# Up projection in Strassen's seven products of half matrices over both token groups, output projection with 512 columns into six open accumulators

## The chip, the cores and the metric

The kernel runs on one core of a Trainium2 chip. The metric is the device time of one execution in microseconds (us); lower is better. The engines are TensorE (PE, with its weight loads as PEld), VectorE (DVE), ScalarE (ACT), GpSimd (POOL) and SyncE (SP); SP's queue issues all the DMAs of this kernel.

## What is computed

One layer of an encoder on two sequences, 512 and 1024 tokens of width 1024, in float32. The kernel puts them together as 1536 tokens. Cut to what matters here:

```python
def trunk(x, ...):
    h = x
    h = h + hybrid_mixer(rmsnorm(h, norm_mix_g), ...)      # attention and gated linear attention
    h = h + sq_relu_mlp(rmsnorm(h, norm_mlp_g), w_up, w_down)
    return rmsnorm(h, norm_final_g)

def hybrid_mixer(u, ...):
    ...
    merged = sigmoid(gate_na) * (na_o @ w_br_na) + sigmoid(gate_gla) * (gla_o @ w_br_gla)
    return merged @ w_out                                  # 1024 x 1024

def sq_relu_mlp(u, w_up, w_down):                          # 1024 x 4096, 4096 x 1024
    return square(relu(u @ w_up)) @ w_down
```

Every matrix product is taken as three: each operand is split into a high part (rounded to float32r) and a low part (what is left), and high x high, high x low and low x high are added up in PSUM.

## The kernel before

The first 900 us (input projections, gated linear attention, neighbourhood attention) are not touched. What follows works on two groups of 768 tokens (`GT`), `for g in range(2)`, and within a group in four stages:

- **Branches** (lines 1311 to 1339): for each of 8 blocks of 128 output columns, four PSUM units of 12 matmuls with 384 columns (two branches, two halves of the tokens, tags d, a, c, b in turn). DVE multiplies each by its gate, adds the two, ACT makes the high part `mh`, DVE the low part `ml`.
- **Output projection** (`wout_mm`, lines 1349 to 1369): for each of six blocks of 128 tokens and four blocks of 256 columns, one PSUM unit of 24 matmuls with 256 columns; DVE adds the result to the row `h`. The last of the four column blocks is taken from a second ring (`dn`) so that a row can be finished, normed (`norm_a`, `norm_b`) and transposed (`x2`, calling `transp_tile`, lines 189 to 198) while the next is computed. `transp_tile` transposes on PE, and ACT and DVE split the result from PSUM into `x2h`, `x2l`.
- **Up projection** (`up`, lines 1394 to 1408): for each of 32 blocks of 128 hidden columns and each half of the tokens, one unit of 24 matmuls with 384 columns in a bank of tag d; ACT takes the Relu out of PSUM, DVE squares it. After every second block `left_factors` forms four sums and differences on DVE and stores seven factors.
- Beside it run the loading of the next group's branch operand (`prep_side`), the sums of down weights (`t_load`, `t_sums`) and, at the end of the second group, the first operands of the down projection (`d_start`).

The **down projection** (`d_all`) already works by Strassen's seven products, reading the factors stored before: 14 steps of 6 units of 24 matmuls with 512 columns, two units ahead prepared by `a_prep` and `b_prep`.

The order of work is written out by hand: the schedule is manual, so each engine runs its instructions in the order in which the program emits them, and the tile framework adds the waits that the data need. Weights come through a ring (`Ring`): SP loads 128x1024 blocks, two of them raw; ACT copies the high part (line 51) and DVE subtracts for the low part (line 52), three of them split. The same split for other tiles is `split_act` (lines 156 and 157). A PSUM tag has a number of banks which its tiles take in turn: two each for tags a, b, c and d here.

Of the kernel before, what the change touches and what calls it, by code (L numbers as in the profile page):

```python
# [79 lines left out]
def tile_trunk(ctx: ExitStack, tc: tile.TileContext, d: dict, y: bass.AP):  # L80
# [64 lines left out]
    for g in range(2):  # L145
        for i in range(8):
            add(f"br{g}.{i}", d["wbr"][i])
        for i in range(3):
            add(f"out{g}.{i}", d["wout"][2 * i], d["wout"][2 * i + 1])
        for i in range(32):  # L150
            add(f"up{g}.{i}", d["wup"][i])
# [880 lines left out]
    axe, ax = right("ax")  # L1032
    x_, h_ = {}, {}

    def big(pool, tag, nm):
        return [pool.tile([128, 8, GT], F32R, tag=tag, bufs=2, name=f"{nm}{c}") for c in "hl"]

    def prep_side(g, pool, tag, xrp, xtag, nb, ahead):

        base = g * GT  # L1040
        x_[g] = big(pool, tag, f"x{g}")
# [4 lines left out]
        def load(e):  # L1046
# [3 lines left out]
            t = xrp.tile([128, 512 if g == 0 else 1024], F32, tag=xtag, bufs=nb, name=f"xr{g}{e}")[:, :512]  # L1050
# [6 lines left out]
        for e in range(ahead):  # L1057
            load(e)
        yield 1
        for e, (kind, i) in enumerate(todo):  # L1060
            t = ld.pop(e)
            if kind == "n":
                sl = slice(i % 2 * 384, i % 2 * 384 + 384)
                split_act(xh[:, i // 2, sl], xl[:, i // 2, sl], t[:, :384])
            else:
# [4 lines left out]
                split_act(xh[:, 4:8, sl], xl[:, 4:8, sl], p.rearrange("p (k t) -> p k t", k=4))  # L1070
            load(e + ahead)
            yield 1

    xre, xr = right("xr")
    pr = prep_side(0, ax, "actA", xr, "xr", 6, 6)
# [10 lines left out]

    p2e = ExitStack()
    p2 = p2e.enter_context(tc.tile_pool(name="p2", bufs=1))
    wde, wd = right("wd")
    dn = Ring(nc, wd, "draw", 1, wd, "dn", 2, [a for _ in range(2) for a in [d["wout"][6], d["wout"][7]]])  # L1090
    dn.load()

    def load_h(g):
        h_[g] = []
        for t in range(6):
            x = p2.tile([128, 1024], F32, tag=f"h{t}", name=f"h{g}{t}")
            SP.dma_start(x, d["x"][g * GT + t * 128:g * GT + (t + 1) * 128])
            h_[g].append(x)

    def load_g(pool, nm, g):  # L1100
        t = pool.tile([128, 1024], F32, tag="gn", name=f"{nm}{g}")
        SP.dma_start(t, d[nm])
        return t
# [13 lines left out]


# [3 lines left out]
    Ad = {(i, kh, g): dr.tile([3, 128, 8, 128], F32, name=f"ad{i}{kh}{g}") for i in LEFT for kh in range(2) for g in range(2)}  # L1122

# [12 lines left out]


# [5 lines left out]
    D1, D2 = [None], [None]  # L1143
    Araw, Ahl, Bhl = {}, {}, {}

    def a_load(u):
        if u < len(units):
            s, t = units[u]
            (i, _, _), kh = steps[s]
            x = D1[0].tile([128, 8, 128], F32R, tag="al", bufs=4, name=f"al{u}")  # L1150
            SP.dma_start(x.bitcast(F32), Ad[i, kh, t // 3][t % 3])
            Araw[u] = x

    def a_prep(u):
        if u < len(units):
            lo = Araw.pop(u)
            hi = D1[0].tile([128, 8, 128], F32R, tag="ah", bufs=4, name=f"ah{u}")
            A.activation(hi, lo.bitcast(F32), AF.Copy)  # L1158
            V.tensor_tensor(lo, lo.bitcast(F32), hi.bitcast(F32), op=ALU.subtract)  # L1159
            Ahl[u] = hi, lo  # L1160

    Braw = {}

    def b_load(s, jj):
# [8 lines left out]
        pool = D1[0] if s == 0 else D2[0]  # L1173
        x = pool.tile([128, 512], F32, tag="bq", bufs=2 if s == 0 else 12, name=f"bq{s}{jj}")
# [3 lines left out]
    def b_prep(s, jj):  # L1178
        if s >= 14:
            return  # L1180
        pool = (D1, D2)[s % 2][0]
        hi = pool.tile([128, 512], F32R, tag="bh", bufs=8, name=f"bh{s}{jj}")
        lo = pool.tile([128, 512], F32R, tag="bl", bufs=8, name=f"bl{s}{jj}")
        split_act(hi, lo, Braw.pop((s, jj)))
        Bhl[s, jj] = hi, lo

    def t_load(j, pool, tags):

        x = [pool.tile([128, 1024], F32, tag=tags[e], bufs=2 if tags[0] == "dnh" else 4, name=f"tq{j}{e}") for e in range(2)]
        for e in range(2):  # L1190
            SP.dma_start(x[e], d["wdn"][2 * j + e])
        return x

    def t_sums(j, x):

        b11, b12, b21, b22 = x[0][:, :512], x[0][:, 512:], x[1][:, :512], x[1][:, 512:]
        V.tensor_tensor(b11, b12, b11, op=ALU.subtract)
        V.tensor_tensor(b12, b22, b12, op=ALU.subtract)
        V.tensor_tensor(b22, b22, b11, op=ALU.subtract)
        V.tensor_tensor(b21, b21, b22, op=ALU.subtract)  # L1200
        for e in range(2):
            SP.dma_start(t_d[2 * j + e], x[e])

    def d_start(part):
        if part == 0:
            for u in range(4):
                a_load(u)
        if part < 4:
            b_load(0, 2 * part)
            b_load(0, 2 * part + 1)  # L1210
        if part > 0:
            b_prep(0, 2 * part - 2)
            b_prep(0, 2 * part - 1)
        if part in (2, 3):
            a_prep(part - 2)

    def d_all():
        hb, acc, ssa = ([], []), {}, {}
        gf = []

        def fin(t, rh, last=False):
# [3 lines left out]
            x = D2[0].tile([128, 1024], F32, tag="x", bufs=3, name=f"xf{t}{rh}")  # L1225
            if rh:
                ss = D2[0].tile([128, 1], F32, tag="ss", bufs=4, name=f"sf{t}")
# [329 lines left out]
```

## Time and profile before

| what | value |
|---|---|
| median of three runs | 2212.14 us (2211.51 to 2214.27) |
| the profiled execution | 2209.44 us |
| its span | 2207.4 us |
| PE busy | 2186.7 us, 99% |
| DVE, ACT busy | 1174.2 us (53%), 782.8 us (35%) |
| branches, per group | 67 us |
| output projection, per group | 73 us |
| up projection, first and second group | 272 and 270 us |
| down projection to the end | 464 us |

Busy time of PE counts the time in which any of its matmuls is in flight. Matmuls are pipelined, so the duration that a matmul's row shows is longer than its distance to the next; what a matmul costs is that distance. Idle time is put down to the instruction that ended it. The stages in the table are stretches of the span, read from the first and last matmuls of their lines.

### The profile page before, as it was taken

How to read it: one execution, taken by the hardware profiler on the slowest of the kernel's cores; microseconds unless marked ns; L12 is line 12 of the kernel's file. 1: busy time of each engine (PE TensorE's matmuls, PEld its weight loads, DVE VectorE, ACT ScalarE, POOL GpSimd, SP SyncE). 2: the span in 40 equal slices, each digit the busy share in tenths (PEclk: the TensorE clock that was granted, in tenths of full speed). 3: DMA queues.
4: the chain of work that ended last, by engine and by line, in shares of the span. 5: the costliest groups of instructions: out<-in, count | busy, mean ns of one | idle time of the engine just before them, and what ended most of it. 6: DMA issues, size and time to landing. Idle time of an engine off the chain costs nothing.

```text
span 2207.4 us, 33043 instructions
## 1 busy us (share of the span) xinstructions
PE 2186.7 (99%) x12864; PEld 2001.6 (91%) x12864; DVE 1174.2 (53%) x2171; ACT 782.8 (35%) x1464; POOL 64.9 (3%) x92
## 2 busy tenths in 40 slices
PE   8999999999999999999999999999999999999998
PEld 8899998888888888899999999999999988888887
DVE  7463876567356666363455454544554544433643
ACT  6622232423355555442322223332222333333542
POOL 1020200000100000000000000000000000000000
PEclk9999999999999999999999999999999999999999
DMA  5342335453377675552477667326777765454653
GB/s 203 124 141 70 102 115 157 100 149 90 118 221 235 203 219 164 198 186 68 164 250 248 215 205 245 105 90 205 227 227 242 248 214 185 166 177 157 210 172 115
DMA packets 256572, 382.45 MB, mean 173 GB/s; under 512 B 35872, under 2 KB 163872, under 8 KB 256416
## 3 DMA queue, kind: packets, MB, share of 16 engines
q1 hardware_dynamic: 256416, 380.35, 53.9%
q8 instruction: 101, 1.65, 0.3%
q14 instruction: 55, 0.45, 0.1%
HBM read 256.54 MB, written 123.73 MB: 172 GB/s over the span
## 4 chain that ended last, share of the span: by engine, by line
PE 90%; issue 7%; DVE 1%; ACT 1%; DMA 1%; POOL 0%; SPq 0%; DVEq 0%; POOLq 0%; ACTq 0%
PE psd L1404 8%; PE psd L1405 8%; PE psd L1403 8%; PE psd L226 7%; PE psd L228 7%; PE psd L227 7%; PE psa L617 3%; PE psd L251 3%; PE psd L252 2%; PE psd L253 2%; PE psd L1364 2%; PE psd L1366 2%; PE psd L1365 2%; PE psc L964 2%; PE psa L1269 2%
## 5 line engine op out<-in xcount | busy, mean ns | idle before, releaser
L52 DVE TENSOR_TENSOR wl<-wr,wh 128x1024 fp32r<-128x1024 f32 x130 | 159.0, 1225 | 149.1 <-ACT wh L51 147.8
L1407 ACT ACTIVATE r<-psd 128x384 f32<-128x384 f32 x128 | 62.9, 492 | 389.8 <-PE psd L1405 389.8
L1408 DVE TENSOR_TENSOR r<-r 128x384 f32<-128x384 f32 x128 | 71.2, 557 | 234.4 <-ACT r L1407 234.4
L51 ACT ACTIVATE wh<-wr 128x1024 fp32r<-128x1024 f32 x130 | 136.7, 1054 | 131.5 <-PE psd L1366 54.0
L226 PE MATMUL psd<-uhiS,wh 128*128 128x512 f32 x448 | 180.6, 403 | 0.8 <-ACT st L288 0.8
L1159 DVE TENSOR_TENSOR al<-al,ah 128x1024 fp32r<-128x1024 f32 x84 | 102.6, 1223 | 148.0 <-ACT ah L1158 148.0
L228 PE MATMUL psd<-uhiS,wl 128*128 128x512 f32 x448 | 175.5, 392 | 0.0
L227 PE MATMUL psd<-uloS,wh 128*128 128x512 f32 x448 | 174.7, 390 | 0.0
L1403 PE MATMUL psd<-n0h,wh 128*128 128x384 f32 x512 | 171.7, 335 | 0.2 <-ACT n0h L197 0.2
L1403 PE MATMUL psd<-n1h,wh 128*128 128x384 f32 x512 | 171.3, 335 | 0.5 <-ACT r L1407 0.3
L1404 PE MATMUL psd<-n0l,wh 128*128 128x384 f32 x512 | 171.1, 334 | 0.3 <-DVE n0l L198 0.3
L1404 PE MATMUL psd<-n1l,wh 128*128 128x384 f32 x512 | 171.1, 334 | 0.3 <-DVE n1l L198 0.3
L1405 PE MATMUL psd<-n0h,wl 128*128 128x384 f32 x512 | 171.1, 334 | 0.0
L1405 PE MATMUL psd<-n1h,wl 128*128 128x384 f32 x512 | 171.0, 334 | 0.0
L1158 ACT ACTIVATE ah<-al 128x1024 fp32r<-128x1024 f32 x84 | 88.6, 1057 | 219.4 <-DMA al<-ads 133.6
L226 PEld LDWEIGHTS psd<-uhiS,wh 128*128 128x128 f32 x448 | 84.2, 188 | 19.0 <-ACT st L288 1.2
L228 PEld LDWEIGHTS psd<-uhiS,wl 128*128 128x128 f32 x448 | 84.0, 188 | 18.5
L227 PEld LDWEIGHTS psd<-uloS,wh 128*128 128x128 f32 x448 | 84.3, 188 | 16.0
L1403 PEld LDWEIGHTS psd<-n1h,wh 128*128 128x128 f32 x512 | 96.1, 188 | 1.1 <-ACT r L1407 0.6
L1404 PEld LDWEIGHTS psd<-n0l,wh 128*128 128x128 f32 x512 | 96.1, 188 | 0.5 <-DVE n0l L198 0.5
L1404 PEld LDWEIGHTS psd<-n1l,wh 128*128 128x128 f32 x512 | 96.1, 188 | 0.5 <-DVE n1l L198 0.5
L1403 PEld LDWEIGHTS psd<-n0h,wh 128*128 128x128 f32 x512 | 96.1, 188 | 0.5 <-ACT n0h L197 0.5
(452 smaller groups left out, 5671.4 us busy)
## 6 DMA issues: line engine op xcount, KB each, us to landing
wr<-in_wup_dram SPq DMA_DIRECT2D x64, 512.0 KB
ads<-s SPq DMA_DIRECT2D x128, 192.0 KB
al<-ads SPq DMA_DIRECT2D x48, 512.0 KB
ad<-r SPq DMA_DIRECT2D x96, 192.0 KB
al<-ad SPq DMA_DIRECT2D x36, 512.0 KB
tq<-in_wdn_dram SPq DMA_DIRECT2D x32, 512.0 KB
t_d<-tq SPq DMA_DIRECT2D x32, 512.0 KB
bq<-t_d SPq DMA_DIRECT2D x64, 256.0 KB
```

The costliest lines, as they stand in the source:

```text
L51: self.nc.scalar.activation(hi, t, AF.Copy)
L52: self.nc.vector.tensor_tensor(lo, t, hi.bitcast(F32), op=ALU.subtract)
L226: T.matmul(p, wh, xh[:, k, sl], start=(k == 0), stop=False)
L227: T.matmul(p, wh, xl[:, k, sl], start=False, stop=False)
L228: T.matmul(p, wl, xh[:, k, sl], start=False, stop=(k == 7))
L251: T.matmul(p[:, :256], xh, wh, start=(k == 0), stop=False)
L1158: A.activation(hi, lo.bitcast(F32), AF.Copy)
L1159: V.tensor_tensor(lo, lo.bitcast(F32), hi.bitcast(F32), op=ALU.subtract)
L1403: T.matmul(p[:, :384], wh[:, es], x2h[:, k, sl], start=(k == 0), stop=False)
L1404: T.matmul(p[:, :384], wh[:, es], x2l[:, k, sl], start=False, stop=False)
L1405: T.matmul(p[:, :384], wl[:, es], x2h[:, k, sl], start=False, stop=(k == 7))
L1408: V.tensor_tensor(r, r, r, op=ALU.mult)
```

## The change

The loop over the two groups is taken apart into branches 0, output 0, branches 1, output 1, and then the up projection of both groups in a row (`up_all`); every group's norm and transposes move into the stage after it, and other work is placed by hooks between blocks (`hook_b0`, `hook_w0`, `hook_b1`, `hook_w1`) and by a table of functions to be called after a given product (`side`).

The output projection (`wout`) holds six PSUM banks open, one for each block of 128 tokens, and passes over the eight rows of weights with 512 columns each; the eight weights are now cut as 256 rows x 512 columns.

The up projection takes a pair of hidden blocks (256 columns) at a time in seven products of half matrices: half of the 1024 rows, one block of 128 columns, half of the tokens. Each is 12 matmuls of 384 columns. The seven left factors of the activations (`factors`, `part`) are made once for each group; the seven right factors of the weights are made in `u_prep`, four products ahead. The sums between products are left to PSUM: product 2 is added onto product 0 in its bank, and so on, and ACT copies the intermediate values out between.

```diff
@@ output projection @@
+    def wout(g, hook):
+        mh, ml = m_[g]
+        for n in range(2):
+            for kq in range(4):
+                wi = where[f"out{g}"] + n * 4 + kq
+                ring.fill(wi)
+                if kq == 0:
+                    acc = [ps("aabbcc"[t]) for t in range(6)]
+                wh, wl = ring.get(wi)
+                for t in range(6):
+                    sl = slice(t * 128, t * 128 + 128)
+                    for kk in range(2):
+                        k = kq * 2 + kk
+                        es = slice(kk * 512, kk * 512 + 512)
+                        a, b = mh[k // 4][:, k % 4, sl], ml[k // 4][:, k % 4, sl]
+                        T.matmul(acc[t], a, wh[:, es], start=(k == 0), stop=False, skip_group_check=True)
+                        T.matmul(acc[t], a, wl[:, es], start=False, stop=False, skip_group_check=True)
+                        T.matmul(acc[t], b, wh[:, es], start=False, stop=(k == 7), skip_group_check=True)
+                    if kq == 3:
+                        hs = h_[g][:, t, n * 512:n * 512 + 512]
+                        V.tensor_tensor(hs, acc[t], hs, op=ALU.add)
+                hook(n * 4 + kq)
@@ norm and transposes, each called from a hook or from side @@
+    def square(g, t, half):
+        s = p2.tile([128, 1], F32, name=f"ss{g}{t}{half}")
+        A.activation(ps("d"), h_[g][:, t, half * 512:half * 512 + 512], AF.Square, accum_out=s)
...
+    def trans_h(g, t):
+        for half in range(2):
+            pt = ps("d")
+            for k in range(4):
+                T.transpose(pt[:, k * 128:(k + 1) * 128], h_[g][:, t, (half * 4 + k) * 128:(half * 4 + k + 1) * 128], ident)
+            A.activation(st_[g][:, t // 3 * 2 + half, :, t % 3 * 128:t % 3 * 128 + 128], pt.rearrange("p (k t) -> p k t", k=4), AF.Copy)
+    def hook_b1(i):
...
+        if i < 6:
+            square(0, i, 1)
+        if 0 < i < 7:
+            norm_h(0, i - 1)
+        if i > 1:
+            trans_h(0, i - 2)
...
@@ factors @@
+    BANK = (0, 1, 0, 2, 0, 1, 0)
+    def part(g, i, src, e):
+        if e == 0:
+            c_[g, i] = q12([2, 4, 384], f"c{g}{i}")
+        c, ks = c_[g, i], slice(2 * e, 2 * e + 2)
+        A.activation(c[:, 0, ks], src, AF.Copy)
+        V.tensor_tensor(c[:, 1, ks], src, c[:, 0, ks].bitcast(F32), op=ALU.subtract)
...
+    def u_prep(n):
+        if n >= 224:
+            return
+        p, i = divmod(n, 7)
+        x = uraw[p]
+        b11, b21, b12, b22 = x[0][:, :512], x[0][:, 512:], x[1][:, :512], x[1][:, 512:]
+        src = (b11, b11, b11, b21, b12, b22, b21)[i]
+        op = {1: (b11, b12, b11), 2: (b11, b22, b11), 4: (b12, b22, b12), 6: (b21, b21, b11)}.get(i)
+        if op:
+            V.tensor_tensor(*op, op=ALU.subtract)
+        if n % 2 == 0:
+            utile[0] = [rngp.tile([128, 1024], F32R, tag=f"w{c}", bufs=3, name=f"uw{c}{n}") for c in "hl"]
...
+        split_act(hi, lo, src)
+        uhl[n] = hi, lo
+        if i == 6:
+            uraw.pop(p)
+            u_load(p + 2)
@@ up projection @@
+    def up_all(side):
+        tail = [None]
+        for n in range(224):
+            p, i = divmod(n, 7)
...
+            b = BANK[i]
+            new = b not in bank
+            if new:
+                bank[b] = ps("abc"[b])[:, :384]
+            wh, wl = uhl.pop(n)
+            c = c_[g, i]
+            for k in range(4):
+                es = slice(k * 128, k * 128 + 128)
+                T.matmul(bank[b], wh[:, es], c[:, 0, k], start=(new and k == 0), stop=False, skip_group_check=True)
+                T.matmul(bank[b], wh[:, es], c[:, 1, k], start=False, stop=False, skip_group_check=True)
+                T.matmul(bank[b], wl[:, es], c[:, 0, k], start=False, stop=(k == 3), skip_group_check=True)
+            if i == 0 and tail[0]:
+                tail[0]()
+            elif i == 1:
+                A.activation(sc[:, :384], bank[0], AF.Copy)
+            elif i == 2:
+                A.activation(sc[:, 384:], bank[1], AF.Copy)
+            elif i == 3:
+                A.activation(sd[:, :384], bank[0], AF.Copy)
+            elif i == 4:
...
+                V.tensor_tensor(re[:, :384], bank[2], sc[:, :384], op=ALU.add)
+                A.activation(re[:, :384], re[:, :384], AF.Relu)
+                A.activation(re[:, :384], re[:, :384], AF.Square)
+            elif i == 5:
+                V.tensor_tensor(ro[:, 384:], bank[0], sc[:, 384:], op=ALU.add)
+            elif i == 6:
+                V.tensor_tensor(ro[:, :384], bank[1], sd[:, :384], op=ALU.add)
+                A.activation(ro, ro, AF.Relu)
+                A.activation(ro, ro, AF.Square)
+                def end(g=g, j=j, re=re, ro=ro, x=bank[0]):
+                    A.activation(re[:, 384:], x, AF.Relu)
+                    A.activation(re[:, 384:], re[:, 384:], AF.Square)
+                    left_factors(g, j, re, ro)
+                tail[0] = end
+            u_prep(n + 4)
+            for f in side.get(n, ()):
+                f()
+        tail[0]()
```

The functions in `side` are: for the first group's last three factors, pair 0; stores, squares, norms and transposes of the second group's rows, pairs 0 to 8; the second group's factors, pairs 9 to 13 (sums and differences of 768 elements) and 15 (twelve calls of `part`); seven rounds of `t_load` and `t_sums`, pairs 10 to 26; the down projection's first operands, pairs 20 to 31. Of the down projection only units 0 and 1 have their left operands before it starts; units 2 and 3 are loaded at its start. The first group's branch operand is loaded four tiles ahead instead of six.

## Rows read from the trace of the kernel before

**Rows 1.** The page: busy time and its share by engine; TensorE's granted clock.

```profile
PE 2186.7 (99%) x12864; PEld 2001.6 (91%) x12864; DVE 1174.2 (53%) x2171; ACT 782.8 (35%) x1464; POOL 64.9 (3%) x92
PEclk9999999999999999999999999999999999999999
```

**Rows 2.** Stretches: length; busy and (instructions) of PE, PEld, DVE, ACT, POOL; clock.

```profile
989.20:1062.20 73.00, 73.00 (x610) 72.74 (x610) 30.23 (x46) 19.17 (x31) 2.77 (x5) 1.00 0.15 51
1062.20:1333.80 271.60, 271.07 (x1578) 270.30 (x1577) 136.51 (x208) 72.02 (x117) 0.55 (x1) 1.00 0.71 226
1333.80:1400.50 66.70, 66.70 (x387) 66.70 (x386) 42.46 (x74) 28.89 (x40) 0.00 (x0) 1.00 0.69 234
1400.50:1473.50 73.00, 73.00 (x610) 72.74 (x609) 30.23 (x46) 19.18 (x31) 2.74 (x5) 1.00 0.13 44
1473.50:1743.00 269.50, 268.69 (x1553) 267.80 (x1553) 133.38 (x200) 69.31 (x109) 0.55 (x1) 1.00 0.70 225
```

**Rows 3.** Timeline of PE: start, duration, instruction; 15 matmuls apart, down projection.

```profile
1896.96 0.39 PE L1268 MATMUL psc<-bh,ah 128*128 128x512 f32 x1
...
1900.36 0.39 PE L1268 MATMUL psc<-bh,ah 128*128 128x512 f32 x1
```

**Rows 4.** Chain of work, whole span: eight transposes of a normed row.

```profile
1450.11 0.87 PE psb L194 x8
```

**Rows 5.** Groups by line and shape, ACT and DVE: busy us, mean ns; idle.

```profile
L156 ACT ACTIVATE bh<-bq 128x512 fp32r<-128x512 f32 x112 | 64.0, 617 | 16.9 <-DMA bq<-in_wdn_dram 16.8
L1407 ACT ACTIVATE r<-psd 128x384 f32<-128x384 f32 x128 | 62.9, 492 | 389.8 <-PE psd L1405 389.8
L1116 ACT ACTIVATE sg<-sg 128x768 f32<-128x768 f32 x32 | 26.6, 843 | 31.9 <-DMA sg<-gate_d 30.9
L1334 ACT ACTIVATE m0h<-sg 128x384 fp32r<-128x384 f32 x16 | 8.3, 524 | 21.2 <-DVE sg L1333 21.2
...
L157 DVE TENSOR_TENSOR bl<-bq,bh 128x512 fp32r<-128x512 f32 x112 | 72.3, 685 | 11.4 <-ACT bh L156 11.4
L1130 DVE TENSOR_TENSOR s<-r,r 128x384 f32<-128x384 f32 x32 | 17.7, 553 | 0.1
L1200 DVE TENSOR_TENSOR tq<-tq 128x512 f32<-128x512 f32 x16 | 11.1, 693 | 0.5
L1332 DVE TENSOR_TENSOR sg<-psa,sg 128x384 f32<-128x384 f32 x16 | 8.8, 551 | 10.5 <-ACT sg L1116 10.5
```

**Rows 6.** Chain of work from 1714 to 1727 us: start, length, what.

```profile
1717.62 7.75 DMA bq<-in_wdn_dram
...
1725.40 0.63 ACT bh L156
1726.04 0.39 ACT r L1407
...
1726.46 0.45 PE psd L1403
```

**Rows 7.** Timelines of ACT and DVE in three stretches: steps one behind the other.

```profile
84.19 1.06 ACT L530 ACTIVATE zt<-zt 128x1024 f32<-128x1024 f32 x1
85.28 1.15 ACT L531 ACTIVATE zt<-zt,one 128x1024 f32<-128x1024 f32 x1
...
1713.73 0.49 ACT L1407 ACTIVATE r<-psd 128x384 f32<-128x384 f32 x1 [2.72 <-PE psd L1405]
...
1714.26 0.56 DVE L1408 TENSOR_TENSOR r<-r 128x384 f32<-128x384 f32 x1
...
1727.73 0.56 DVE L1130 TENSOR_TENSOR s<-r,r 128x384 f32<-128x384 f32 x1
1728.33 0.56 DVE L1131 TENSOR_TENSOR s<-s,r 128x384 f32<-128x384 f32 x1
1728.80 0.55 DVE L1132 TENSOR_TENSOR s<-r 128x384 f32<-128x384 f32 x1
```

**Rows 8.** Groups by line and shape, ACT: reading the sum of a square.

```profile
L733 ACT ACTIVATION_READ_ACCUMULATOR jk1S<-psb 128x1 f32 x16 | 3.1, 196 | 0.0
```

## What the change does to the time: the prediction

> **What bounds the kernel now.** I read the busy times first: TensorE (PE) is busy 99% of the span, DVE 53%, ACT 35%, at the full clock [rows 1]. An average says nothing of one stage, so next the stretches that the change rewrites: output projection, up projection and branches, per group [rows 2]. In each PE's busy time is the stretch to within 0.8 us, while ACT and DVE have half of it or less. So what counts there is matmuls times their spacing, and whatever makes PE wait. Durations of PE rows are latencies (a 384-column matmul shows 0.33 us); the spacing comes from counts: the second group's branch stage runs 384 matmuls of 384 columns in 66.70 us, 0.1737 us each [rows 2]. With 512 columns, 15 steps take 3.40 us, 0.2267 each [rows 3]. With 256 columns: 73.0 us hold 576 matmuls and 32 transposes at 0.109 (eight in 0.87 us), so 0.1207 each [rows 2, 4].
>
> **The gain on PE.** Up projection: before 2 groups x 32 blocks x 2 halves x 24 = 3072 matmuls of 384 columns; after 2 x 16 pairs x 7 products x 12 = 2688. 384 fewer x 0.1737 = 66.7 us. Output projection: 1152 x 0.1207 = 139.0 us become 576 x 0.2267 = 130.6: 8.4 us. The 96 transposes of the normed rows remain, at the same price, in other stages. Small waits at the old stage borders go: 0.8 + 0.5 us in the up stretches [rows 2]. Together 76.5 us, if PE never waits.
>
> **What the products ask of ACT and DVE.** A product lasts 12 x 0.1737 = 2.08 us, a pair of blocks (seven products) 14.6 us. Per pair DVE now has seven low parts (0.685), four differences of weights (0.69), three adds from PSUM (0.55) and four left factors (0.55): 11.4 us; ACT has seven high parts (0.62), three copies and a Relu from PSUM (0.49 each), three more passes of 384 (0.52) and two of 768 (0.84): 9.6 us [rows 5]. Both fit into 14.6 us. But they stand in one queue each, and the order in it matters: four of the seven weights go DVE, ACT, DVE, with DVE held while ACT works, and the copies that free a bank stand behind them.
>
> That a queued instruction blocks ready ones is in the trace: the copy bh waited 7.75 us for its transfer, the Relu emitted behind it on ACT ran only after it, and PE's next matmul waited for that Relu [rows 6].
>
> **The chain of one pair.** Bank 0 takes products 0, 2, 4 and 6. Product 2 may not start before ACT has copied out product 0; that copy is emitted after product 1, behind everything emitted before. Time 0 is product 3's sum standing in PSUM. Waits across engines cost 0.04 us (ACT 1713.73 + 0.49, DVE starts 1714.26), so do dependent steps on one engine (ACT 84.19 + 1.06, next 85.28; DVE 1727.73 + 0.56, next 1728.33); independent ones overlap by 0.08 to 0.1 (DVE 1728.33, next 1728.80) [rows 7]. The durations are those above:
> - re: add 0.59, Relu 1.15, Square 1.71; ACT's high part of the weight two products on 2.23; DVE's low part 2.95;
> - product 4's add 3.42 (the sum stood ready at 2.1); difference 4.03, high 4.69, low 5.42;
> - product 5's add 5.89; Relu over 768 6.77, Square 7.65; high part 8.17;
> - product 6's Relu 8.56 (ready at 6.3), Square 9.12; left factors s1 9.71, s2 10.31, s3 10.78, s4 11.25;
> - difference 11.86, high 12.52, and only then the copy of bank 0: 12.91.
>
> PE, not stopped, would want product 2 at 5 x 2.08 - 0.16 = 10.24 us. It gets it at 12.95, so it waits 2.7 us in every pair but the first: 31 x 2.7 = 84 us. If waits cost 0.06 us it is 2.9 per pair; if a dependent step on the same engine could start like an independent one it is about 2.0. Bounds 62 to 90 us; I take 84, as its steps are the rows'.
>
> After that copy the loop has almost no slack: ACT and DVE end product 3's share some 0.3 us before product 3's sum is there. So what else is put into these queues lengthens the loop. Piece by piece, by DVE's time in queue: seven rounds of down-weight sums (4 x 0.72 = 2.9 each, 2.3 after the slack) 16 us; 22 factor pieces of 768 elements for the second group (0.87 each, slack off) 17; first down operands (eight of 512, two of 1024) 7; norm, squares, transposes and last factors of the first nine pairs 7. Sum 47 us. Below, 20, if half of it falls into DVE's waits for ACT; above, their whole DVE time, 62. I take 47: most are emitted just ahead of an add or a low part.
>
> **Other places.** (a) Second branch stage: the square of a half row is written into a bank of tag d, of which there are two, and the second transposes of the same step need that bank. PE's last unit of a block ends; multiply, add (0.55 and 0.59), ACT's copy 0.56, square about 0.6, reading its sum 0.2 [rows 5, 8]: 2.5 us, of which four transposes cover 0.4. Four blocks (2 to 5) x 2.1 = 8.6 us; between 0 (another bank) and 10. (b) The first branch operand is loaded four ahead, not six: 0 to 4 us, I take 1. (c) Start of the down stage: blocks 2 and 3 load only when the last factors are issued. They have two units, 2 x 24 x 0.2267 = 10.9 us; the factors take about 4, transfer 4 to 8 (the longest row: 7.75 [rows 6]), split 2.3. 0 to 4 us, I take 1. (d) On SP's queue the same bytes of weights and factors pass as before; a pair's weights are asked for eight products (17 us) ahead against that 7.75: nothing, so long as no store before them waits longer than 9 us. (e) Output projection: six open sums; each is added out by DVE five units before its bank is wanted, nothing. Its ring needs one split in 8.2 us (1.05 and 1.23): covered. Nine of the sixteen rounds of down-weight sums (two loads, four DVE steps, two stores each) move into the output and branch stages. Such a round can hold DVE until its load has landed behind six row loads on SP; behind it on DVE stand ring splits, due two items (16 us) later, and the adds of the fourth item: nothing, 5 us if the loads are late. The norm's power on POOL now has four products or a whole branch block until its use: nothing.
>
> **Sum.** The profiled execution took 2209.4 us, 2.0 more than its span. 2209.4 - 76.5 + 84 + 47 + 8.6 + 1 + 1 = 2274.5. The median shown is 2.7 above the profiled execution: 2277 us, 2.9% slower.
>
> **A rule weighed.** In the up stretches PE had everything and DVE half [rows 2]; by the count above DVE would have 11.4 of 14.6 us. The Trainium skill (Perfetto Trace Analysis, "Identifying the Most-Contended Engine") takes the engine with the highest occupancy for the bottleneck; by that PE would stay the bound and the time would be the first rival's. Against it stands the wait of [rows 6], on an ACT that was idle most of that stretch. The same page ("Matmuls") wants independent groups to rotate through banks, so that evacuation overlaps the next group; the branch stage does, and shows no wait [rows 2]; products 0, 2, 4 and 6 don't.
>
> **Rivals.**
> 1. *Covered* (faster). The copies of bank 0 come in time, because the loop through ACT and DVE is under 10.24 us a pair: my 12.9 would have to be 2.7 too long. For it: both engines have room on average. Against: every step is a measured row, and the order is that of the code. 2212.1 - 76.5 + 5 (parts a to c, small) = 2141. It decides at 10.24 us: above, each 0.1 us costs 3.1; the gain is eaten when the stall averages 2.4 us over 31 pairs.
> 2. *Lower bounds* (slower by little): dependent steps overlap and half of the side work hides. 2212.1 - 76.5 + 62 + 20 + 6 = 2224.
> 3. *Transfers too*: weights or stores on SP come late on top of the chain, one wait of 2 us in every second pair and more at the start of down: 2277 + 16 x 2 + 8 = 2317.
> 4. *Not done as said*: the compiler keeps fewer waits than the code's order implies, so product 2 doesn't wait for the copy. Bank 0 is read and then accumulated into, so a wait must be there; under 1 in 100, time as in 1.
>
> **Chances.** Forecast 0.70, first rival 0.13, second 0.12, third 0.05. The range takes in the forecast with its bounds (84 and 47 down to 62 and 30, up to 90 and 62) and the second rival: 2215 to 2308. Faster by over 0.2% (about what a measurement of this kernel can tell from no change) 0.13, within it 0.03, slower 0.84.
>
> **What would show it.** Right: PE waits in the up projection for ACT's copy of sc, once a pair, 2 to 3 us, most at the start of product 2; PE's busy share of that stretch about 78%, its length near 600 us instead of 541; the longest waits around pair 15, where twelve factor pieces stand; matmul spacing unchanged; output projection about 65 us a group; four waits of 2 us between blocks of the second branch stage. Wrong: PE busy over 97% in the up projection (then ACT or DVE took the steps faster or in another order), or PE waiting there for weights that come from a transfer.

## The result and the profile after

The changed kernel takes 2339.5 us (2334.6 to 2342.6) against 2212.2: 1.057 times as long, interval 1.0548 to 1.0595. The forecast was slower, 2277 us; the time lies 62 us above it and 31 above its range. The profiled execution took 2342.6 us, its span is 2340.8.

The profile after, which stands beside [rows 1] and [rows 2]: the page's busy times and granted clock; then six stretches (start:end, length, busy time and count of PE, PEld, DVE, ACT and POOL, granted clock, share of the transfer engines, GB/s): first branch stage, its output projection, second branch stage, its output projection, up projection, down projection; then what PE waited for (in all, times, longest).

```profile
PE 2188.2 (93%) x11904; PEld 1958.6 (84%) x11904; DVE 1332.3 (57%) x2423; ACT 966.3 (41%) x1848; POOL 65.3 (3%) x92
PEclk9999999999999999999999999889989999999999
```

```profile
927.40:1009.70 82.30, 71.04 (x410) 70.66 (x409) 47.87 (x82) 35.32 (x54) 0.00 (x0) 0.94 0.56 176
1009.70:1075.00 65.30, 65.30 (x290) 54.05 (x289) 27.32 (x36) 16.45 (x30) 0.00 (x0) 1.00 0.67 238
1075.00:1162.40 87.40, 77.03 (x427) 75.56 (x426) 54.41 (x84) 36.90 (x65) 4.08 (x6) 0.94 0.56 196
1162.40:1228.40 66.00, 66.00 (x296) 54.77 (x295) 43.99 (x57) 21.84 (x39) 0.00 (x0) 1.00 0.65 239
1228.40:1869.50 641.10, 530.91 (x2738) 515.49 (x2737) 398.42 (x640) 311.69 (x566) 4.05 (x6) 0.91 0.49 148
1869.50:2340.80 471.30, 463.51 (x2017) 378.06 (x2015) 206.19 (x245) 161.72 (x243) 6.58 (x12) 1.00 0.53 180
```

```profile
PE psa L1323 <- ACT sc L1329: 87.5, 30, 3.9
PE psa L1323 <- DVE ro L1341: 21.4, 15, 4.9
PE psb L1071 <- DMA xr<-go_d: 11.6, 2, 11.3
PE psd L1175 <- ACT psd L1157: 9.0, 4, 3.1
```

PE was busy 99% of the time and is now idle 7% of it, most of that in the up projection and the two branch stages. The first line of waits is the one that the forecast named: product 2 of a pair (L1323) waits until ACT has copied product 0 out of the bank into the tile sc, 30 times, 2.9 us each on average.

How such a wait comes about is seen on the two engines' own timelines, here of the pair at 1655 us (start, duration, instruction, idle before it and what ended it). ACT first, then DVE:

```profile
1653.21 0.53 ACT L1349 ACTIVATE re<-re 128x384 f32<-128x384 f32 x1
1656.49 0.63 ACT L153 ACTIVATE uwh<-ux 128x512 fp32r<-128x512 f32 x1 [2.75 <-DVE ux L1282]
1657.03 0.47 ACT L1329 ACTIVATE sc<-psa 128x384 f32<-128x384 f32 x1
```

```profile
1653.77 0.56 DVE L1299 TENSOR_TENSOR s<-re,ro 128x384 f32<-128x384 f32 x1 [0.24 <-ACT re L1349]
1654.36 0.56 DVE L1300 TENSOR_TENSOR s<-s,re 128x384 f32<-128x384 f32 x1
1654.84 0.55 DVE L1301 TENSOR_TENSOR s<-re 128x384 f32<-128x384 f32 x1
1655.31 0.55 DVE L1302 TENSOR_TENSOR s<-ro,s 128x384 f32<-128x384 f32 x1
1655.77 0.69 DVE L1282 TENSOR_TENSOR ux<-ux 128x512 f32<-128x512 f32 x1
```

ACT stands idle for 2.75 us in front of the high part of a weight (L153). That part needs the difference L1282, which stands in DVE's queue behind the four left factors (L1299 to L1302), which needed ACT's Square (L1349). Only behind the high part comes the copy that PE has waited for all along. And this is what PE does then:

```profile
1657.55 0.69 PE L1323 MATMUL psa<-c,uwh 128*128 128x384 f32 x1 [2.89 <-ACT sc L1329]
1658.04 0.52 PE L1324 MATMUL psa<-c,uwh 128*128 128x384 f32 x1
1658.36 0.52 PE L1325 MATMUL psa<-c,uwl 128*128 128x384 f32 x1
...
1661.10 0.33 PE L1323 MATMUL psc<-c,uwh 128*128 128x384 f32 x1
1661.27 0.33 PE L1324 MATMUL psc<-c,uwh 128*128 128x384 f32 x1
```

Behind the wait the matmuls start 0.32 us apart, from the tenth on 0.17 again. The granted clock of the first ones is 0.50 (1.2 GHz, the lower of the two levels), of the last ones 1.00 (2.4 GHz). Below, half clock means 0.50. In the kernel before the granted clock was full in every slice [rows 1]; here it is 0.91 on average over the up projection.

**Where 133 us of span went.** The starts of successive matmuls in the up projection divide it. 2688 matmuls at 0.1737 and 48 transposes at 0.109 would take 472.1 us. Steps longer than 0.36 us hold 122.8 us beyond that (63 steps: the waits), steps of 0.25 to 0.36 hold 45.4 us more than at full clock (325 matmuls at half clock), together 640. The stretch's 641.1 us are 100 more than the 541.1 of the two stretches before [rows 2]. The first branch stage takes 82.3 us (66.6 before, from the starts of its matmuls), the second 87.4 (66.7, [rows 2]), the output projections 65.3 and 66.0 (73.0, [rows 2]); the down projection is 6.9 us longer, and the part ahead of the branches 4.6. In that part one wait of PE at 337 us, which took 2.3 us with the full clock after it, now takes 3.1 us with half clock after it.

### The profile page after: what moved, and what is told of

Its sections match the earlier page's. It is cut to its first block, busy times and chain, and to the rows that moved or that the text cites. A ratio compares the mean times of both kernels' runs of the same rounds, so it can differ in the third digit from the quotient of the medians.

```text
span 2340.8 us, 31809 instructions
## 1 busy us (share of the span) xinstructions
PE 2188.2 (93%) x11904; PEld 1958.6 (84%) x11904; DVE 1332.3 (57%) x2423; ACT 966.3 (41%) x1848; POOL 65.3 (3%) x92
## 5 line engine op out<-in xcount | busy, mean ns | idle before, releaser
L1323 PE MATMUL psa<-c,uwh 128*128 128x384 f32 x512 | 192.3, 376 | 109.9 <-ACT sc L1329 87.5
L154 DVE TENSOR_TENSOR uwl<-ux,uwh 128x512 fp32r<-128x512 f32 x224 | 155.0, 692 | 217.9 <-ACT uwh L153 217.6
L153 ACT ACTIVATE uwh<-ux 128x512 fp32r<-128x512 f32 x224 | 139.7, 624 | 192.8 <-DVE ux L1282 163.5
L1323 PEld LDWEIGHTS psa<-c,uwh 128*128 128x128 f32 x512 | 106.8, 209 | 124.7 <-ACT sc L1329 96.6
L1324 PE MATMUL psa<-c,uwh 128*128 128x384 f32 x512 | 187.3, 366 | 0.3 <-DVE c L1242 0.3
L1325 PE MATMUL psa<-c,uwl 128*128 128x384 f32 x512 | 186.6, 364 | 0.0
L153 ACT ACTIVATE ah<-al 128x1024 fp32r<-128x1024 f32 x82 | 86.6, 1058 | 233.1 <-DMA al<-ads 137.9
L52 DVE TENSOR_TENSOR wl<-wr,wh 128x1024 fp32r<-128x1024 f32 x70 | 85.5, 1223 | 129.1 <-ACT wh L51 118.5
L51 ACT ACTIVATE wh<-wr 128x1024 fp32r<-128x1024 f32 x70 | 73.8, 1056 | 143.0 <-PE psc L1199 63.4
L1324 PEld LDWEIGHTS psa<-c,uwh 128*128 128x128 f32 x512 | 107.7, 210 | 0.7 <-DVE c L1242 0.7
L1325 PEld LDWEIGHTS psa<-c,uwl 128*128 128x128 f32 x512 | 108.2, 211 | 0.0
L248 PE MATMUL psd<-wh,uhiS 128*128 128x256 f32 x320 | 93.5, 292 | 3.1 <-DVE sv L314 3.1
L250 PE MATMUL psd<-wh,uloS 128*128 128x256 f32 x320 | 91.2, 285 | 0.0
L249 PE MATMUL psd<-wl,uhiS 128*128 128x256 f32 x320 | 91.2, 285 | 0.0
L223 PE MATMUL psd<-uhiP,wh 128*128 128x512 f32 x224 | 90.8, 405 | 0.0
```

Source lines behind the costliest of these rows:

```text
L52: self.nc.vector.tensor_tensor(lo, t, hi.bitcast(F32), op=ALU.subtract)
L153: A.activation(hi, src, AF.Copy)
L154: V.tensor_tensor(lo, src, hi.bitcast(F32), op=ALU.subtract)
L223: T.matmul(p, wh, xh[:, k, sl], start=(k == 0), stop=False)
L248: T.matmul(p[:, :256], xh, wh, start=(k == 0), stop=False)
L249: T.matmul(p[:, :256], xh, wl, start=False, stop=False)
```

## The experiments

The theory: what costs time is the order in ACT's and DVE's queues, and PE's idleness in turn costs clock. The rivals: ACT and DVE have too much to do whatever the order; the clock falls for another reason; side work or transfers do it by themselves. Four kernels first.

**Filling the waits.** Behind product 1:

```diff
+            if i == 1 and 8 <= p < 32:
+                dm = ps("d")[:, :384]
+                for k in range(4):
+                    ... the three matmuls of product 1 once more, into dm
```

> The changed kernel with 12 more matmuls a pair in pairs 9 to 31, put right behind product 1, where PE waits for ACT's copy of sc; they repeat product 1 into a spare bank that nothing reads (23 x 12 = 276 matmuls, 48 us of PE time at 0.1737 us). Theory (the waits come from the order of the ACT and DVE queues, and the granted clock falls because PE stands idle in them): the fillers lie inside the waits, the chain behind the waits is as long as before, and the granted clock stays full in pairs 9 to 31; the 32 us that the half-clock matmuls cost there go, so 2339 - 25 to 32 = 2307 to 2315 us. Rival A (PE's own work is the bound, or the clock falls for the amount of work and not for idleness): the 48 us come on top, 2387 us. Rival B (the clock falls for a reason that has nothing to do with PE's idleness): the fillers are hidden and nothing else changes, 2339 us with about as many half-clock matmuls in the up stretch as now (324).

(The loop begins at pair 8: 24 pairs, 288 fillers, 50.0 us.) Measured: 2318.1 us, ratio 1.048 (1.0464 to 1.0495). The up stretch, and the waits for the same two copies (here at other line numbers):

```profile
1225.90:1843.60 617.70, 551.90 (x3025) 535.62 (x3024) 398.12 (x640) 309.78 (x565) 4.07 (x6) 0.97 0.51 153
```

```profile
PE psa L1323 <- ACT sc L1336: 39.4, 29, 3.5
```

PE does 288 matmuls more and the stretch is 23 us shorter. The waits fell by 47.2 us, which is what the fillers took up to 3 us. The half-clock matmuls of pairs 9 to 31 cost 8.5 us instead of 32.5. Work that nobody needs has paid for itself through the clock: it was the idleness that lowered it. Both rivals fall (2387 and 2339 us). At 21 us the gain is below the 25 to 32 expected: 25.7 us of half clock went, but 2.8 us of the fillers were not covered, and the rest is within what runs differ by.

**The difference one product earlier.** The first difference of a pair gets a tile of its own:

```diff
+        if i == 0:
+            ud[p] = ...
+        d1 = ud[p]
-        src = (b11, b11, b11, b21, b12, b22, b21)[i]
-        op = {1: (b11, b12, b11), 2: (b11, b22, b11), 4: (b12, b22, b12), 6: (b21, b21, b11)}.get(i)
+        src = (b11, d1, b11, b21, b12, b22, b21)[i]
+        op = {p == 0: (d1, b12, b11), 1 + (p == 0): (b11, b22, d1), 3: (b12, b22, b12), 5: (b21, b21, b11)}.get(i)
```

> The changed kernel with one thing moved: the subtraction that makes a product's weight difference goes into DVE's queue one product earlier, ahead of the previous split, so that ACT's copy of the split finds it done (the first difference of a pair gets a tile of its own, so that none overwrites what is still to be split; pair 0 stays as it is in its first two). The number of instructions on ACT, DVE and PE is the same. Theory (the queue order: ACT's copy of sc stands behind a split that waits for DVE's subtraction, which stands behind DVE's left factors): pairs without side work run without a wait (14.6 us a pair), the gaps in the up stretch fall from about 128 us to about 36, most half-clock matmuls go (45 us to 10 to 15), the up stretch takes 505 to 525 us instead of 641, the kernel 2205 to 2225 us. Rival (ACT and DVE are simply too busy for the shorter PE time): the same instructions take as long, 2325 to 2340 us.

Measured: 2209.2 us, ratio 0.9989 (0.9979 to 0.9998): 130 us faster than the change as it came, with the same number of instructions. Its up stretch and its longest wait:

```profile
1226.40:1734.40 508.00, 481.61 (x2737) 475.73 (x2736) 387.86 (x640) 306.31 (x566) 4.39 (x6) 0.99 0.61 187
```

```profile
PE psa L1326 <- DVE ro L1344: 26.4, 17, 4.8
```

The waits for sc are gone; what is left (17 waits for DVE's sum ro) lies in the pairs with side work or right behind them. The stretch and the kernel's time lie in the expected ranges; waits (29.8 us, expected 36) and half clock (7.0, expected 10 to 15) came out below. ACT's and DVE's load was not the limit: DVE is busy for 388 of 508 us.

**The borders**, three edits in three stretches:

```diff
-        for _ in range(2):
+        for _ in range(2 if i else 1):
             next(pr, 0)
...
-        if i < 6:
-            square(0, i, 1)
         if 0 < i < 7:
             norm_h(0, i - 1)
         if i > 1:
             trans_h(0, i - 2)
+        if i < 6:
+            square(0, i, 1)
...
-                ss = D3[0].tile([128, 1], F32, tag="ss", bufs=4, name=f"sf{t}")
+                ss = D3[0].tile([128, 1], F32, tag="ss", bufs=8, name=f"sf{t}")
...
```

> The changed kernel with three small edits outside the up projection, each in its own stretch. (1) First branch stage: the second group's operand loads are issued behind block 0 and its first tile is transposed behind block 1, not in the same block. Expected: PE's wait of 11.3 us at 936 us and the half clock behind it go, the stretch takes 68 to 70 us instead of 82.3. Rival (the load is late for the traffic of that stage, not for its place): the wait moves to the next block and stays above 5 us. (2) Second branch stage: the square of a block goes behind the transposes of the block instead of ahead of them, so that no transpose takes the bank that the square holds. Expected: the four waits (9.0 us) and most of the half-clock stretches go, 73 to 77 us instead of 87.4. Rival (ACT is too busy there): the waits stay. (3) Down projection: four more small tiles in the pool D3, which moves the right operands of the even steps by 128 bytes. If the place in memory makes their matmuls 0.233 us apart instead of 0.227, the spacing of the even steps becomes 0.227 and the stretch 5 to 6 us shorter; if the cause is what runs beside them, nothing changes. Sum: 2339 - 12 - 12 - 6 = 2309 us, 2300 to 2318.

Measured: 2313.3 us, ratio 1.0459 (1.0439 to 1.0478). First branch stage, second, down projection, and the waits that are left in the first:

```profile
927.10:1000.20 73.10, 69.69 (x410) 69.10 (x409) 47.20 (x81) 35.25 (x53) 0.00 (x0) 1.00 0.63 198
...
1065.50:1140.10 74.60, 72.66 (x434) 71.43 (x433) 54.39 (x86) 36.62 (x65) 3.63 (x6) 1.00 0.65 229
...
1851.00:2316.70 465.70, 457.57 (x2016) 377.88 (x2015) 206.25 (x245) 161.64 (x243) 6.58 (x12) 1.00 0.54 182
```

```profile
PE psb L1071 <- DMA xr<-go_d: 2.4, 1, 2.4
PE psb L1071 <- DVE sg L1137: 1.0, 1, 1.0
```

(1) The stage is 9.2 us shorter, not 12 to 14: 2.4 us of waiting for the load stay, below the rival's 5, so it was mostly the load's place. What the 2.4 us come from isn't shown. (2) and (3) as expected: 12.8 and 5.6 us. What held up the second stage was the order in which the users of one bank stood; the down projection is taken up below. (The up projection, which the edits don't touch, took 645.5 us in the profiled execution here, with 50.6 us of half clock instead of 45.4. The runs of one kernel differ by as much: 2308.7 to 2318.5 us here.)

**Side work on another engine.** The seven rounds of down-weight sums, on POOL:

```diff
-    def t_sums(j, x):
+    def t_sums(j, x, E=V):
...
-        at(p + 1, 3, lambda j=j: t_sums(j, tq["tw"]))
+        at(p + 1, 3, lambda j=j: t_sums(j, tq["tw"], G))
```

> The changed kernel with the seven groups of four subtractions of the down weights that lie in the up projection (0.795 us each, 22 us) moved from DVE to POOL, which has 3% of work. Theory (side work in DVE's queue lengthens the chain to ACT's copy): the gaps fall by some 15 to 19 us, the clock gives some 3 to 5 us more, 2314 to 2322 us. Rival (the side work is hidden, and the waits of those pairs have another cause): 2335 to 2342 us. Second rival (POOL and DVE get in each other's way): DVE's own instructions in those pairs take longer than now (0.54 to 0.69 us), and the gain is lost or turns into a loss, 2340 to 2355 us.

Measured: 2338.1 us, ratio 1.0568 (1.0551 to 1.0584): no gain. Waits 122.4 us, half clock 45.8, as without the edit. But they are other waits: those for ro fell from 21.4 to 7.5 us, those for sc rose from 87.5 to 102.6. One round, POOL above, DVE below:

```profile
1436.48 1.28 POOL L1222 TENSOR_TENSOR tw<-tw 128x512 f32<-128x512 f32 x1 [155.79 <-DVE uwl L154]
1437.85 1.62 POOL L1223 TENSOR_TENSOR tw<-tw 128x512 f32<-128x512 f32 x1
```

```profile
1436.33 0.55 DVE L1341 TENSOR_TENSOR ro<-psa,sc 128x384 f32<-128x384 f32 x1
1436.80 1.52 DVE L1282 TENSOR_TENSOR ux<-ux,ux 128x512 f32<-128x512 f32 x1
1439.02 1.00 DVE L154 TENSOR_TENSOR uwl<-ux,uwh 128x512 fp32r<-128x512 f32 x1 [0.70 <-ACT uwh L153]
```

While POOL works, DVE's difference takes 1.52 us instead of 0.68 and its low part 1.00 instead of 0.69; the sum that reads one operand from PSUM keeps its 0.55. The side work was not hidden, since the waits for ro fell without it; the second rival's mechanism is seen in these rows. That it alone made the waits for sc longer fits the sum, but wasn't tested apart. The Trainium skill (SBUF — State Buffer, "SBUF: two separate sides") says that a DVE operation with two inputs in SBUF and a GpSimd operation that reads SBUF take a shared read port in turn; the rows agree: the difference ends 0.56 us after POOL's first subtraction, the low part 0.55 after its second.

**A few lines moved.** The cheapest change of order, without another tile:

```diff
+            if i in (0, 6):
+                u_prep(n + 4)
             if i == 0 and tail[0]:
                 tail[0]()
...
-            u_prep(n + 4)
+            if i not in (0, 6):
+                u_prep(n + 4)
```

> The changed kernel with one call moved by a few lines: behind products 0 and 6 of a pair the weight preparation (difference and split) goes into the queues ahead of the pair's own work (the tail's squares and left factors; the last sum ro and its squares), not behind it. Everything else is as in the change, the difference still right ahead of its split. Theory (order in the queues): by the queue's arithmetic a pair without side work keeps about 1.1 us of waits instead of 2.7 to 3.1, the gaps of the up stretch fall from 128 us to about 75, the half-clock matmuls' 45 us to 20 to 35, the up stretch takes 560 to 580 us, the kernel 2260 to 2280 us. Rival (it is the number of steps from DVE to ACT and back, not their order, that PE waits for): within 15 us of 2339 us.

Measured: 2249.0 us, ratio 1.0164 (1.0147 to 1.0181), below the expected range; waits 58.3 us (expected 75), half clock 19.7.

```profile
1225.30:1775.30 550.00, 500.25 (x2737) 484.68 (x2736) 390.82 (x641) 306.06 (x565) 4.11 (x6) 0.97 0.57 172
```

```profile
PE psa L1323 <- ACT sc L1331: 11.5, 13, 2.1
```

The number of hand-overs between DVE and ACT is the same as in the change; their order is worth 90 us. Most of the waits that are left are for DVE's sum ro (35.1 us, 19 times). The queue arithmetic is right in kind and too high by 17 us here.

**All together.** The difference ahead, the border edits, and the side work spread out:

```diff
...
-        at(p + 1, 3, lambda j=j: t_sums(j, tq["tw"]))
+    ts = [(p, 6) for p in range(9, 14)] + [(14, 1), (14, 6), (17, 1), (17, 6)]
+    ts += [(p, i) for p in range(18, 27) for i in (1, 6)] + [(27, 1)]
...
+        for e in range(4):
+            at(*ts[4 * (j - 9) + e], lambda j=j, w=w, e=e: t_sums(j, tq["tw"][w], (e,)))
...
+    next(pr)
     br(0, hook_b0)
```

> The difference ahead of the split (as measured alone: up stretch 508 us) and the three edits at the borders, the first of them carried on (the loads of the second group's operand go out ahead of block 0, its first tile is transposed behind block 1), and one edit more: the 28 subtractions of the down weights that lie in the up projection stay on DVE, but no longer four in a row: one or two a pair, behind products 1 and 6, in pairs 9 to 14 and 17 to 27, with a second buffer for the loads. Theory: the waits for DVE's sum ro (26 us) are the side work in DVE's queue; by the queue's arithmetic the gaps fall by 11 us and the clock gives some 2 to 3 us: up stretch 492 to 497 us; first branch stage 69 to 71 us, second 74 to 76, down 466; in all 2209 - 28 - 2 - 13 = 2166 us, 2158 to 2176. Rival (those waits have another cause, the side work only sits beside it): up stretch 506 to 510, 2179 us.

Measured: 2170.7 us (2167.9 to 2170.8), ratio 0.9809 (0.9795 to 0.9824): 1.9% faster than the kernel before, 7% faster than the change as it came. First branch stage, second, up, down, and the waits:

```profile
927.10:1001.70 74.60, 71.05 (x410) 70.71 (x409) 47.14 (x81) 35.27 (x53) 0.00 (x0) 0.98 0.62 194
...
1067.00:1141.20 74.20, 72.59 (x432) 71.36 (x431) 54.28 (x85) 36.63 (x65) 3.63 (x6) 1.00 0.65 231
...
1206.60:1703.20 496.60, 481.21 (x2738) 474.89 (x2738) 382.96 (x640) 306.55 (x566) 4.41 (x6) 0.99 0.63 191
1703.20:2169.00 465.80, 457.73 (x2017) 378.15 (x2016) 206.24 (x245) 161.76 (x243) 6.60 (x12) 1.00 0.54 182
```

```profile
PE psa L1325 <- DVE ro L1343: 14.4, 15, 3.2
PE psb L1071 <- DVE sg L1137: 3.5, 1, 3.5
```

The up projection came in at the forecast, and so did the waits (18.3 us, 11.5 less than with the difference alone): so what was left there was in large part side work standing in a row in DVE's queue. The first branch stage missed its 69 to 71 us: with the loads of the second group out first, PE waits 3.5 us for DVE's use of the gates instead of 2.4 for the load. That fits loads that now stand ahead of the gates' on SP, but this wasn't followed up.

**The down projection's spacing.** In the changed kernel the matmuls of the even steps, whose right operands lie in the pool D3, start further apart than before [rows 3], those of the odd steps don't. Even and odd step, twelve matmuls apart:

```profile
2009.69 0.39 PE L1482 MATMUL psa<-bl,ah 128*128 128x512 f32 x1
...
2012.49 0.39 PE L1482 MATMUL psa<-bl,ah 128*128 128x512 f32 x1
...
2042.64 0.39 PE L1483 MATMUL psa<-bh,al 128*128 128x512 f32 x1
...
2045.36 0.39 PE L1483 MATMUL psa<-bh,al 128*128 128x512 f32 x1
```

2.80 us are 0.233 each, 2.72 are 0.227. The third edit above moved D3 by 128 bytes and made all steps 0.227. In the kernel before, both operands of all its steps start at the same place modulo 256 bytes; in the changed kernel the right operands of the even steps lie 128 bytes off (places as the build of the programs gives them). Three kernels, each run once, followed up on it. In the first, each tile of the contraction starts 32 bytes further on than the one before:

```diff
-            hi = pool.tile([128, 512], F32R, tag="bh", bufs=8, name=f"bh{s}{jj}")
+            hi = pool.tile([128, 576], F32R, tag="bh", bufs=8, name=f"bh{s}{jj}")[:, 8 * jj:8 * jj + 512]
...
```

> The changed kernel with the right operands of the down projection from step 1 on in tiles that are 256 bytes longer, and the operand of the contraction's tile jj (0 to 7) starting 32 x jj bytes into its tile. In the pool D2 (odd steps) the starts modulo 256 bytes are then 224, 0, 32, ..., 192, in D3 (even steps) 96, 128, ..., 64; without it they are 224 in D2, where matmuls follow each other by 0.227 us, and 96 in D3, where it is 0.233. If the start address sets the spacing, it depends on jj in the same way in both pools for the same start (0.227 at 224, 0.233 at 96, the others show which part of the address counts). If the pool or the step sets it, odd steps have 0.227 and even ones 0.233 for all jj. In time nothing to speak of: 2339 us +- 10.

Measured: 2345.7 us; from step 1 on all steps average 0.2325 us. Equal starts have equal spacings in both pools (a tile at 96: behind its three matmuls 233, 229, 238 ns in D2 and 233, 230, 236 in D3), so neither pool nor step is the cause. But a tile at 224 has 234, 230, 231 ns here and not 227: the right operand's own start is not the whole of it. So the left operand was moved:

```diff
...
-                hi, lo = D2[0].tile([128, 8, 128], F32R, tag="ah", bufs=4, name=f"ah{u}"), x.bitcast(F32R)
+                hi, lo = D2[0].tile([128, 1088], F32R, tag="ah", bufs=4, name=f"ah{u}")[:, 32:1056].rearrange("p (k c) -> p k c", k=8), x.bitcast(F32R)
```

> The changed kernel with the left operands of the down projection (al and ah, the stationary side) 128 bytes further on in memory, at 96 modulo 256 bytes instead of 224; the right operands stay at 224 (odd steps) and 96 (even steps). If the spacing of these matmuls hangs on the two operands' addresses relative to each other, the steps change places: odd steps 0.233 us, even steps from step 2 on 0.227. If it hangs on the right operand's address alone, nothing changes: odd 0.227, even 0.233. Step 0 has operands of its own and tells nothing. Time 2339 us +- 10 by either.

Even and odd step, twelve matmuls apart:

```profile
2007.67 0.39 PE L1482 MATMUL psa<-bl,ah 128*128 128x512 f32 x1
...
2010.39 0.39 PE L1482 MATMUL psa<-bl,ah 128*128 128x512 f32 x1
...
2039.83 0.39 PE L1482 MATMUL psa<-bl,ah 128*128 128x512 f32 x1
...
2042.63 0.39 PE L1482 MATMUL psa<-bl,ah 128*128 128x512 f32 x1
```

The steps have changed places: 2.72 and 2.80 (2340.1 us in all). And with only the right operands moved, by 64 bytes:

> The changed kernel with the right operands of the down projection 64 bytes further on in tiles that are 256 bytes longer: at 32 modulo 256 bytes in odd steps and 160 in even ones, all of a step alike. If the address modulo 128 bytes were what counts, odd and even steps have one and the same spacing; if modulo 256, they may differ, and both are new points beside 224 (0.227 us) and 96 (0.233). Time 2339 us +- 10.

Measured: 2337.9 us; 0.229 us in the odd steps (right operand at 32, left at 224), 0.233 in the even ones (160 and 224). So the two operands' places relative to each other count: 0.227 at the same place modulo 256 bytes, 0.229 to 0.233 at the three other distances tried. Why, and why a mixture as in the first of the three is slow even for tiles at the same place, stays open.

## Why the prediction was wrong, point by point

Waits and half clock in the up projection, counted as above:

| kernel | up stretch, us | waits, us (steps) | half clock, us (matmuls) |
|---|---|---|---|
| the change | 641.0 | 122.8 (63) | 45.4 (325) |
| waits filled | 617.7 (with 50.0 of fillers) | 75.6 (54) | 19.7 (149) |
| split first | 550.0 | 58.3 (46) | 19.7 (150) |
| difference ahead | 508.0 | 29.8 (19) | 7.0 (55) |
| all together | 496.6 | 18.3 (17) | 7.0 (56) |

- *Gain on PE, 76.5 us*: right. Without waits and half clock the up projection has 472 us of work and took 496.6 in the combined kernel, of which 25 are waits and half clock; the output projections take 65.3 and 66.0, about as said.
- *Chain 84 us and side work 47*: right in mechanism, and 131 in all against 122.8 measured. Pairs 18, 19 and 29, with no side work in their part of the queues, wait 2.8, 2.7 and 2.7 us by the starts of the matmuls, where 2.7 was said. Over 31 pairs that is the chain's 84, and some 38 are left for the side work instead of 47. The longest waits are in pairs 15 and 16 (8.5 and 7.2 us), as forecast.
- *"Matmul spacing unchanged"*: the step that failed. The sum priced a wait at its length. In all five kernels of the table PE lost another 0.2 to 0.4 us of half clock for each us of waiting; here 45 us in the up projection, two thirds of the miss of 68 us against the profiled execution's own time. The rows of the kernel before give no price for it: its clock is full in every slice [rows 1], behind its wait of 2.3 us too. A rival "the waits also cost clock" should have stood there, with the upper bound of the range raised. The Trainium skill describes such a case in another kernel (TensorE: Matmul & The Clock Gate, "A second HAM failure mode: psum-queue depth-cycling"): a TensorE that idles briefly between groups, as it cycles through the banks, goes back and forth between its two clocks. The trace agrees, at 26 stretches of half clock in the up projection.
- *The rest of the 68 us*: 12 in the first branch stage (b), 8 in the second (a, with its half clock), 6 in the down projection (c and the spacing), 5 ahead of the branches; 8 the other way, as the waits of the up projection were shorter than 131.
- *(a) Square's bank, 8.6 us* (four times 2.1 is 8.4): right, four waits, 9.0 us; the clock behind them added about 4 (the edit gave 12.8).
- *(b) First branch operand, 1 us*: wrong place. It was looked for in the first group's operand, for which PE waited 0.4 us. The wait of 11.3 us is for the second group's, whose loads and first transposes were put behind the same block. The loads stand last in SP's queue, and a weight load ahead of them (L43) waited 8.1 us for DVE's low part of an earlier weight (L52):

```profile
939.22 1.22 DVE L52 TENSOR_TENSOR wl<-wr,wh 128x1024 fp32r<-128x1024 f32 x1 [13.60 <-ACT wh L51]
...
940.47 0.33 SPq L43 DMA_DIRECT2D wr<-in_wbr_dram  x1
940.85 0.91 SPq L1103 DMA_DIRECT2D sg<-gate_d  x2
941.80 0.96 SPq L1057 DMA_DIRECT2D xr<-go_d  x2
```

  That low part waited for ACT's high part (L51), which stood in ACT's queue behind the Sigmoid of the gates; ACT had waited 7.0 us for the gates to land. PE had come to the transpose at 936 us; it ran at 947. Point (d), nothing on SP, was argued for weights and factors alone and left these loads out.
- *(c) Start of down, 1 us*: measured 1.4. The other 5.5 us are the spacing above, which the prediction could not know from rows; it took 0.2267 us as a property of the shape [rows 3].
- *What would show it*: waits for sc of 2 to 3 us, about once a pair, came out; "PE's busy share about 78%" did not (530.9 of 641.1 us, 83%). The busy time is 59 us above the work at full clock, 45 of them half clock: such matmuls count as busy. A busy share hides a slow clock, the spacing shows it.
- *Rivals*: "covered" is what the kernel with the difference ahead and the combined one make of the change; 2170.7 us is 2141 plus the waits and half clock that are left in the up projection (25) and 4 more, about what PE waits in the first branch stage. The weighed rule, that the busiest engine is the bound, failed for the change itself as argued: DVE was busy 398 of 641 us, ACT 312, and PE waited for them all the same.
- *Range*: the bounds of its two large terms give 2298, its upper end was 2308; a term that was missing can't lie in it. Less the 45 us of half clock in the up projection, the profiled execution's 2342.6 would be 2297, inside the range.

## What to carry to other kernels

Shortening TensorE's work pays only if what frees its banks keeps up, and that is a matter of the order in two queues rather than of their load: write down one period of both queues with their hand-overs, and emit the producer of a hand-over a step ahead, so that no copy which PE needs stands behind an instruction that still waits for the other engine. Price a recurring wait of PE at its length plus the matmuls at half clock behind it (here 0.2 to 0.4 us for each us), and read spacings, not busy shares. Work on the side goes into such a queue one instruction per period, not in a row.

## What the runs showed of the hardware

- Matmuls of 512 columns start 0.227 us apart with both operands at the same place modulo 256 bytes, and 0.229 to 0.233 at distances of 64, 128 and 192: up to 3%, moved from one half of the steps to the other by shifting either operand. The Trainium skill (SBUF — State Buffer, "Who interferes with whom") gives PE two independent read ports and says that it never waits on anyone; for these operands the measurement says that their places matter.
- With the sums on POOL, DVE's differences of 512 elements, both inputs in SBUF, took 1.3 to 1.7 us beside POOL's subtractions (five of them), 0.68 alone.
- A wait isn't always followed by half clock: in the up projection there were 63 waits and 26 stretches at 0.50. In the kernel before the wait of 2.3 us had none behind it. What decides it wasn't tried beyond the fillers.
